# Pairs of tiles in one DMA for the branch products, block work in single steps, and an earlier start of the next sums' loads

## The chip, the cores and the metric

The kernel runs on one core of a Trainium2 chip. The metric is device time in microseconds (us) of one execution, smaller is better. The engines of the core run side by side, each in its own order: TensorE (PE: matmuls), VectorE (DVE), ScalarE (ACT), GpSimd (POOL) and SyncE (SP), whose queue issues all DMAs of this kernel. An instruction waits on its engine until all it depends on is done, and all that stand behind it wait too.

## What is computed

One layer of a streaming encoder, for 2048 prompt frames and 64 frames of a running stream: an input projection, a differential attention branch, a retention branch, gates, and an output part. The change touches the output part only, which is in the reference:

```python
oa = (rmsnorm(oa, subln_g) * (1.0 - lam_init)).reshape(B, T, W_A) * jax.nn.silu(za)
ob = rmsnorm(ob).reshape(B, T, W_B) * jax.nn.silu(zb)
m = ga * (oa @ w_oa) + gb * (ob @ w_ob)
return x + m @ w_out
```

`oa`, `ob`, `za`, `zb` have 512 columns for 2112 rows, `ga` and `gb` (sigmoids) and `m` 1024 columns, `w_out` is 1024 x 1024. All is float32: each operand is split into a high and a low part, and each product takes three matmuls (high x high, high x low, low x high).

## The kernel before

A planner writes the program. Every piece of work is a generator (a task) with a priority; `loop` runs the task with the lowest priority number among those that are due by the planner's own estimates, `self.pe` being the planned time of TensorE. `yield t` means "go on when TensorE has reached t", `yield lambda: ...` "when this holds", `take`/`give` hand out buffers with the time from which they are free. The order in which tasks emit instructions is the static order of each engine. `ld` (L135) and `st` (L140) are DMAs on SyncE.

The part around the change, in the order of the program:

- **Scratch.** Earlier stages write transposed results to DRAM: `oaT`, `obT` (the branches before their gate), `zaT`, `zbT`, and the merge gates `gaT`, `gbT`.
- **Branch products**, the stage from 1575 to 1773 us. The 2112 rows are cut into 8 groups (g) of 264 columns (`GW`). For each branch (br 0 and 1) and each of four tiles kt of 128 channels, `out_prep` loads the two tiles `on` and `z` (132 KB each) into two of 11 "oz" buffers; `og_fin` does silu on ScalarE (L1664), the product on POOL (L1667), the high part `ogh` on ScalarE (L1677) and the low part `ogl` on VectorE (L1680). The buffer of `z` is given back after the product, that of `on` after the low part. Of `ogh` and `ogl` there are three sets of 4 tiles, so a set can be written only when TensorE is through with the set three before it.
- `m_tile` then makes one of eight tiles (ct) of 128 output channels: 12 matmuls for branch a into a "mm" bank, 12 for branch b into an "s" bank (L1722 to L1724). There are two banks of each. Tile ct of group g needs two gates: `gates` loads them into two of 10 "gt" buffers, `gate` takes tanh on ScalarE (L1698), `m_fin` multiplies both banks with them on VectorE (the eviction, L1742), adds them on POOL (L1746) and stores the sum `mT` (132 KB). One gt buffer is given back after the add, the other when the store is planned to have landed.
- **Weights of the products**: `load_wo` loads 128 x 256 pieces, `split_fin` splits them (L1610, L1613, L1617).
- **Block work for the last matrix.** `w_out` is cut into four block rows c, and the last product uses seven products P1 to P7 of sums of blocks instead of eight of blocks. `b_prep` loads four raw tiles for each c (`b_raw`, 256 KB each), forms the sums t1 to t4 on VectorE (L1758) and splits blocks and sums (`b_split`: casts L1815 on ScalarE, subtractions L1818 on VectorE). The sums of c = 2, 3 are split late (`b_late`), when the buffers of the first product weights come free in group 7. All this runs beside the branch products, on ScalarE and VectorE. `out_prep` waits ahead of the loads of group 1 until the first four raw loads are out (`b_left < 13`).
- **The last matrix**, from 1773 us: for each of 8 groups `y_load` loads four tiles `a` of `mT`, `y_prep` forms the sums s1 to s4 (s1, s2 on VectorE, s3, s4 on POOL) and splits them into `ah` (L1853) and `al` (L1860); `y_group` multiplies (L1934) in the order P1, P2, P6, P5, P7, P3, P4; `y_out` copies banks to `u` (L1962), adds the residual and stores (L1984). For the first group, loads of `a11` and `a12` come early; the others follow when t4 of all four c is split.

Of the kernel before, what the change touches and what calls it, by code (L numbers as in the profile page):

```python
# [8 lines left out]
F32 = mybir.dt.float32  # L9
# [23 lines left out]
BUFS = {"thi": 1, "tlo": 2, "ev": 3, "q": 2, "K": 4, "V": 4, "ath": 2, "atl": 2,  # L33
        "ws": 3, "w": 12, "r_o": 1, "r_sq": 1, "r_y": 1, "r_hi": 1, "r_lo": 1, "state": 2,
        "mm": 2, "s": 2, "at": 2, "pv": 1, "tp": 1,
        "oz": 11, "og": 16, "ob": 8, "gt": 10, "wa": 16, "st": 13, "ac": 16, "u": 9, "xt": 10}
LAT = 250.0
SLACK = 400.0
PACE = 700.0
# [20 lines left out]
class Hybrid:  # L60
# [91 lines left out]
    def scratch(self):  # L152
        tc = self.tc
        self.qT = [tc.dram_tile([4, 128, TT], F32, name=f"qT{i}") for i in range(2)]
        self.kT = [tc.dram_tile([4, 128, TT], F32, name=f"kT{i}") for i in range(2)]
        self.vN = [tc.dram_tile([TT, 512], F32, name=f"vN{i}") for i in range(2)]
        self.vsN = tc.dram_tile([NS, 512], F32, name="vsN")
        self.vbN = tc.dram_tile([TT, 512], F32, name="vbN")
        self.qbT = tc.dram_tile([4, 128, TT], F32, name="qbT")
        self.kbT = tc.dram_tile([4, 128, TT], F32, name="kbT")  # L160
        self.zaT = tc.dram_tile([4, 128, 8 * GW], F32, name="zaT")
        self.zbT = tc.dram_tile([4, 128, 8 * GW], F32, name="zbT")
        self.gaT = tc.dram_tile([8, 128, 8 * GW], F32, name="gaT")
        self.gbT = tc.dram_tile([8, 128, 8 * GW], F32, name="gbT")
        self.oaT = tc.dram_tile([4, 128, 8 * GW], F32, name="oaT")
        self.obT = tc.dram_tile([4, 128, 8 * GW], F32, name="obT")
        self.mT = tc.dram_tile([8, 128, 8 * GW], F32, name="mT")

    def consts(self):
# [1436 lines left out]
    def split_fin(self, tag, h, l, s, t, on_pool, slot, key):  # L1606
# [12 lines left out]
        self.give(tag, t)  # L1619
        slot[key] = t  # L1620

    def load_wo(self, br, q):
        csl = slice(256 * (q % 2), 256 * (q % 2) + 256)
        for kt in range(4):
            hl, slot = self.wo[br][kt]
            h, l = hl[q // 2]
            yield from self.take("oz")
            s = self.sb(self.z3p, [128, GW], "oz", "wst")[:, :256]
            t = self.ld(s, self.i[("w_o_diff", "w_o_ret")[br]][0, 128 * kt:128 * kt + 128, 256 * q:256 * q + 256],
                        1 << 17)  # L1630
            self.spawn(self.split_fin("oz", h[:, csl], l[:, csl], s, t, (kt + q) % 3 == 0, slot, q), 2)
            yield self.pe

    def out_prep(self):
        pa = self.z3p
        self.wo = [[([[self.sb(self.zq, [128, 512], "wa", "woq", F32R) for n in "hl"],
                      [pa.tile([128, 512], F32R, tag=f"wo{n}{br}{kt}", name=f"wo{n}{br}{kt}") for n in "hl"]], {})
                    for kt in range(4)] for br in range(2)]
        for br in range(2):
            yield from self.load_wo(br, 0)  # L1640
        for g in range(8):
            gsl = slice(GW * g, GW * g + GW)
            for br, (oT, zT) in enumerate(((self.oaT, self.zaT), (self.obT, self.zbT))):
                for kt in range(4):
                    yield from self.take("oz", 2)
                    on = self.sb(pa, [128, GW], "oz", "on")
                    z = self.sb(pa, [128, GW], "oz", "z")
                    self.ld(z, zT[kt][:, gsl], 1 << 17)
                    t = self.ld(on, oT[kt][:, gsl], 1 << 17)
                    og = []  # L1650
                    self.ogs.append(og)
                    self.spawn(self.og_fin(on, z, t, og, (2 * g + br) % 3 == 2), 1)
                    yield self.pe
            if g == 0:
                self.spawn(self.gates(), 0)
                for q in range(1, 4):
                    for br in range(2):
                        yield from self.load_wo(br, q)
                yield lambda: self.b_left < 13

    def og_fin(self, on, z, t, og, third):
        nc = self.nc
# [3 lines left out]
        yield t  # L1666
        nc.gpsimd.tensor_mul(on, on, z)  # L1667
        t = self.G(GW, t)
        self.give("oz", t)
        tag = "ob" if third else "og"  # L1670
        yield from self.take(tag, 2)
        pool = self.z4 if third else self.z3p
# [62 lines left out]
    def m_fin(self, g, ct, pss):  # L1735
# [9 lines left out]
        yield t  # L1745
        nc.gpsimd.tensor_add(gs[0], gs[0], gs[1])  # L1746
# [428 lines left out]
    def run(self):  # L2175
# [20 lines left out]
        self.b_left = 16  # L2196
        for k in ("ac", "u", "xt", "ob"):
            self.res[k].free = []
        self.q_end = self.smx = None
# [96 lines left out]
```

## Time and profile before

| | us |
|---|---|
| median of 3 runs | 1947.14 |
| fastest and slowest of them | 1945.34, 1948.15 |
| the profiled execution | 1945.82 |
| its span | 1944.0 |
| branch products in it | 1574.90 to 1773.03 |
| last matrix in it | 1773.03 to the end |

The stages of the tail, each row a stretch: length, then the busy time of TensorE, its weight loads, VectorE, ScalarE and POOL, with the instructions; then the granted TensorE clock (1.00 is full speed), the busy share of the DMA engines, and GB/s.

```
1531.00:1575.00 44.00, 44.00 (x196) 36.44 (x195) 21.32 (x36) 25.78 (x64) 21.03 (x24) 1.00 0.89 273
1575.00:1599.00 24.00, 23.21 (x189) 22.83 (x188) 18.93 (x29) 12.20 (x31) 15.82 (x17) 1.00 0.66 203
1599.00:1624.00 25.00, 24.81 (x204) 24.61 (x203) 18.18 (x34) 14.67 (x35) 16.48 (x18) 1.00 0.87 265
1674.00:1699.00 25.00, 24.37 (x196) 23.81 (x195) 11.07 (x26) 14.89 (x37) 12.84 (x17) 1.00 0.88 258
1723.00:1747.00 24.00, 23.72 (x192) 23.33 (x192) 10.09 (x25) 11.69 (x28) 8.31 (x11) 1.00 0.60 168
```

How to read the views below: a row of the timeline has start, length, engine, line, operation, `out<-in`, shapes, and in brackets the idle time just before it and what ended it. In the list of waits, `<-` names the last releaser. `mm`, `s` and `at` are PSUM banks, `woh`/`woq` product weights, `bh`/`bl` and `bht`/`blt` high and low parts of blocks and of block sums.

### The profile page before, as it was taken

The numbers are of one execution on the slowest core, as the hardware profiler recorded it, in microseconds if no ns is written. First come the engines' busy times: TensorE is split into PE (matmuls) and PEld (weight loads), VectorE is DVE, ScalarE is ACT, GpSimd is POOL, SyncE is SP. The second block draws the span as 40 slices with busy tenths as digits, with TensorE's granted clock in tenths as the row PEclk, the third lists the DMA queues.
The fourth block names the chain that finished last, engine by engine and source line by source line (L and its number), as shares of the span: only waits on it lengthen the run. The fifth ranks groups of instructions, "written<-read, shape, count | busy, mean of one in ns | idle before, by whom it ended". The sixth has DMA issues, their size and how long they took to land.

```text
span 1944.0 us, 33842 instructions
## 1 busy us (share of the span) xinstructions
PE 1927.5 (99%) x11984; PEld 1731.2 (89%) x11984; DVE 1166.6 (60%) x2798; ACT 964.9 (50%) x2072; POOL 490.1 (25%) x429
## 2 busy tenths in 40 slices
PE   9999999999999999999999999999999999999999
PEld 8779999999988899999998888888888889998887
DVE  6753777646666336648856757845773376545643
ACT  7443766544434235535765646544563445653321
POOL 4310112112122121211121111112113356543422
PEclk9999999999999999999999999999999999999999
DMA  7747454335566655654344253363133678866651
GB/s 235 240 151 199 143 143 132 106 102 156 163 192 187 166 148 168 202 183 141 112 120 128 76 146 96 99 185 116 63 99 108 190 229 259 264 196 189 190 151 65
DMA packets 372074, 303.32 MB, mean 156 GB/s; under 512 B 77440, under 2 KB 334720, under 8 KB 371904
## 3 DMA queue, kind: packets, MB, share of 16 engines
q1 hardware_dynamic: 371904, 301.16, 52.6%
q8 instruction: 94, 1.54, 0.4%
q14 instruction: 76, 0.62, 0.1%
HBM read 195.87 MB, written 100.14 MB: 152 GB/s over the span
## 4 chain that ended last, share of the span: by engine, by line
PE 88%; DVE 5%; DMA 3%; POOL 1%; issue 1%; ACT 1%; SPq 1%; DVEq 0%; POOLq 0%; ACTq 0%
PE mm L554 51%; PE mm L1934 4%; PE s L1052 3%; PE s L1053 3%; PE at L1160 3%; PE at L1934 2%; PE pv L1139 2%; PE pv L1140 2%; PE pv L1138 2%; PE s L1934 1%; PE s L1723 1%; PE s L1724 1%; PE pv L1521 1%; PE mm L1723 1%; PE s L1722 1%
## 5 line engine op out<-in xcount | busy, mean ns | idle before, releaser
L514 POOL TENSOR_TENSOR wl<-ws,wh 128x512 fp32r<-128x512 f32 x191 | 261.4, 1380 | 896.2 <-ACT wh L504 544.9
L554 PE MATMUL mm<-xh,wh 128*128 128x512 f32 (+2 forms) x1280 | 460.7, 360 | 0.0
L554 PE MATMUL mm<-xh,wl 128*128 128x512 f32 (+2 forms) x1280 | 452.7, 354 | 0.0
L554 PE MATMUL mm<-xl,wh 128*128 128x512 f32 (+2 forms) x1280 | 451.9, 353 | 0.0
L554 PEld LDWEIGHTS mm<-xh,wl 128*128 128x128 f32 x1280 | 241.0, 188 | 31.7
L554 PEld LDWEIGHTS mm<-xh,wh 128*128 128x128 f32 x1280 | 241.4, 189 | 29.1 <-issue 0.2
L554 PEld LDWEIGHTS mm<-xl,wh 128*128 128x128 f32 x1280 | 241.6, 189 | 27.8
L554 PE MATMUL mm<-wh,xh 128*128 128x256 f32 (+1 forms) x768 | 236.7, 308 | 0.0
L554 PE MATMUL mm<-wh,xl 128*128 128x256 f32 (+1 forms) x768 | 231.3, 301 | 0.0
L554 PE MATMUL mm<-wl,xh 128*128 128x256 f32 (+1 forms) x768 | 231.0, 301 | 0.0
L1175 DVE TENSOR_TENSOR atl<-at,ath 128x512 fp32r<-128x512 f32 (+1 forms) x144 | 93.7, 659 | 136.2 <-ACT ath L1173 136.1
L504 ACT CAST wh<-ws 128x512 fp32r<-128x512 f32 x192 | 117.0, 617 | 112.6 <-PE mm L554 90.3
L1091 ACT ACTIVATE row<-row,a_mx 128x1024 f32<-128x1024 f32 (+7 forms) x160 | 153.7, 962 | 24.5 <-DVE a_mx L1071 24.3
L554 PEld LDWEIGHTS mm<-wh,xh 128*128 128x128 f32 x768 | 146.3, 190 | 7.1 <-issue 0.5
L554 PEld LDWEIGHTS mm<-wl,xh 128*128 128x128 f32 x768 | 146.4, 191 | 6.7 <-issue 0.5
L554 PEld LDWEIGHTS mm<-wh,xl 128*128 128x128 f32 x768 | 146.3, 190 | 5.5
L865 DVE TENSOR_TENSOR ev<-mm,rsb 128x512 f32<-128x512 f32 x140 | 83.0, 593 | 112.8 <-PE mm L554 112.4
L1173 ACT CAST ath<-at 128x512 fp32r<-128x512 f32 (+1 forms) x144 | 78.7, 563 | 141.5 <-PE at L1160 138.4
L1061 DVE CUSTOM_DVE_ANT_0 row<-s,dfar 128x512 f32<-128x512 f32 (+2 forms) x192 | 118.2, 630 | 46.4 <-PE s L1053 45.9
L1052 PE MATMUL s<-K,q 128*128 128x512 f32 (+3 forms) x320 | 118.4, 374 | 0.7 <-DVE a_acc L1061 0.7
L1053 PE MATMUL s<-K,q 128*128 128x512 f32 (+3 forms) x320 | 115.2, 362 | 0.0
L1110 ACT ACTIVATE row<-row,a_w 128x1024 f32<-128x1024 f32 (+4 forms) x96 | 85.1, 898 | 34.4 <-DVE a_w L1105 31.2
(342 smaller groups left out, 4193.5 us busy)
## 6 DMA issues: line engine op xcount, KB each, us to landing
ws<-in_w_in_dram SPq DMA_DIRECT2D x192, 256.0 KB, 3.1
q<-qT SPq DMA_DIRECT2D x128, 128.0 KB, 3.0
V<-vN SPq DMA_DIRECT2D x24, 512.0 KB, 5.4
K<-kT SPq DMA_DIRECT2D x48, 256.0 KB, 4.3
a<-mT SPq DMA_DIRECT2D x34, 256.0 KB, 4.1
gt<-gaT SPq DMA_DIRECT2D x64, 132.0 KB, 3.2
gt<-gbT SPq DMA_DIRECT2D x64, 132.0 KB, 3.1
mT<-gt SPq DMA_DIRECT2D x64, 132.0 KB, 3.0
```

What stands on the lines that cost most here:

```text
L504: self.nc.scalar.copy(h, st)
L514: self.nc.gpsimd.tensor_sub(l, st, h.bitcast(F32))
L554: nc.tensor.matmul(ps, p, q, start=c == 0 and i == 0, stop=c == KC - 1 and i == 2)
L865: nc.vector.tensor_mul(ev, ps, rsb)
L1052: nc.tensor.matmul(ps, q1s, kk, start=True, stop=False)
L1053: nc.tensor.matmul(ps, q2s, kk, start=False, stop=True)
L1061: nc.vector.tensor_tensor_reduce(out=units[k0 // 1024][:, k0 % 1024:k0 % 1024 + n], in0=ps, in1=tab, scale=-SLOPES[h], scalar=3.0e38, op0= ...
L1091: nc.scalar.activation(u, u, AF.Exp, bias=mx, scale=-1.0, accum_out=lp[:, k:k + 1])
L1110: nc.scalar.activation(u1, u1, AF.Identity, scale=w[:, 1:2])
L1173: nc.scalar.copy(ah[:, :w], at[:, :w])
L1175: nc.vector.tensor_sub(al[:, :w], at[:, :w], ah[:, :w].bitcast(F32))
L1934: nc.tensor.matmul(q[b], u, v, start=fresh and c == 0 and m == 0, stop=c == 3 and m == 2, skip_group_check=True)
```

## The change

Three edits go together.

1. The scratch of each branch and of the gates is interleaved (`ozT`, `gT`), so that `on` and `z` of a tile come by one DMA of 264 KB into one double buffer, and both gates too. Buffers: 5 doubles for 11 singles ("oz"), 5 doubles for 10 singles ("gt"). An oz double is given back after the low part, a gt double after the store. The product weights come two pieces to a DMA.
2. `b_raw`, `b_prep` and `b_fin` (for c < 2) yield until 1500 ns of planned TensorE time have passed after each step. The wait on `b_left` goes.
3. `y_load` starts when t1 of three c is split, instead of t4 of all four.

```diff
-        "oz": 11, "og": 16, "ob": 8, "gt": 10, "wa": 16, "st": 13, "ac": 16, "u": 9, "xt": 10}
+        "oz": 5, "og": 16, "ob": 8, "gt": 5, "wa": 16, "st": 13, "ac": 16, "u": 9, "xt": 10}
...
+        self.ozT = [tc.dram_tile([4, 128, 2, 8 * GW], F32, name=f"ozT{br}") for br in range(2)]
+        self.gT = tc.dram_tile([8, 128, 2, 8 * GW], F32, name="gT")
+        (self.oaT, self.zaT), (self.obT, self.zbT) = ([[t[h][:, k] for h in range(4)] for k in range(2)]
+                                                      for t in self.ozT)
+        self.gaT, self.gbT = ([self.gT[c][:, k] for c in range(8)] for k in range(2))
...
-        for kt in range(4):
-            hl, slot = self.wo[br][kt]
-            h, l = hl[q // 2]
+        for k2 in range(2):
             yield from self.take("oz")
-            s = self.sb(self.z3p, [128, GW], "oz", "wst")[:, :256]
-            t = self.ld(s, self.i[("w_o_diff", "w_o_ret")[br]][0, 128 * kt:128 * kt + 128, 256 * q:256 * q + 256],
-                        1 << 17)
+            s = self.sb(self.z3p, [128, 2, GW], "oz", "wst")[:, :, :256]
+            t = self.ld(s, self.i[("w_o_diff", "w_o_ret")[br]][0, 256 * k2:256 * k2 + 256, 256 * q:256 * q + 256]
+                        .rearrange("(c p) n -> p c n", p=128), 1 << 18)
...
-                    yield from self.take("oz", 2)
-                    on = self.sb(pa, [128, GW], "oz", "on")
-                    z = self.sb(pa, [128, GW], "oz", "z")
-                    self.ld(z, zT[kt][:, gsl], 1 << 17)
-                    t = self.ld(on, oT[kt][:, gsl], 1 << 17)
+                    yield from self.take("oz")
+                    both = self.sb(pa, [128, 2, GW], "oz", "oz")
+                    t = self.ld(both, self.ozT[br][kt][:, :, gsl], 1 << 18)
...
-                yield lambda: self.b_left < 13
...
         t = self.G(GW, t)
-        self.give("oz", t)
...
-            yield from self.take("gt", 2)
-            pair = [self.sb(self.z3p, [128, GW], "gt") for _ in range(2)]
-            for gt, gT in zip(pair, (self.gaT, self.gbT)):
-                t = self.ld(gt, gT[ct][:, GW * g:GW * g + GW], 1 << 17)
-            self.spawn(self.gate(n, ct, pair, t), 0)
+            yield from self.take("gt")
+            both = self.sb(self.z3p, [128, 2, GW], "gt")
+            t = self.ld(both, self.gT[ct][:, :, GW * g:GW * g + GW], 1 << 18)
+            self.spawn(self.gate(n, ct, [both[:, br] for br in range(2)], t), 0)
...
         t = self.G(GW, t)
-        self.give("gt", t)
         yield t
         t = self.st(self.mT[ct][:, GW * g:GW * g + GW], gs[0], 1 << 17)
         self.give("gt", t)
...
-            self.b_left -= 1
-        yield t + 600
+            yield self.pe + 1500
+        if t + 600 > self.pe:
+            yield t + 600
...
             t1 = self.add(False, ALU.subtract, raw["t1"], raw["12"], raw["11"], self.pe)
+            yield self.pe + 1500
             for k in ("11", "21", "22"):
                 t = yield from self.b_split(k, c, raw[k], self.pe)
+                yield self.pe + 1500
...
-            yield t3
+            yield max(t3, self.pe + 1500)
...
-            yield t2
+            yield max(t2, self.pe + 1500)
...
             self.give("st", t)
+            if c < 2:
+                yield self.pe + 1500
...
-        yield lambda: len(self.wt["t4"]) == 4
+        yield lambda: len(self.wt["t1"]) > 2
```

TensorE's instructions and their order are the same in both programs, and the other engines have as many as before, but for SyncE, which issues 1410 DMAs instead of 1554: 64 fewer for the gates, 64 for `on` and `z`, 16 for weights. The order of the others differs from about 1527 us on.

ScalarE at the boundary of groups 1 and 2, before (`gt<-gt,bg` is a tanh, `z<-z` a silu, `ogh<-on` the high part that TensorE needs at the boundary, `bht` a block sum's):

```order
L1698 ACTIVATE gt<-gt,bg 128x264 x2
L1664 ACTIVATE z<-z 128x264
L1815 CAST bht_18301<-wst 128x512
L1815 CAST bht_18299<-wst 128x512
L1698 ACTIVATE gt<-gt,bg 128x264 x2
L1815 CAST bht_18303<-wst 128x512
L1677 CAST ogh<-on 128x264 x8
L1664 ACTIVATE z<-z 128x264
```

The same place on ScalarE in the changed program, where `oz<-oz` is the silu and `ogh<-oz` the high part:

```order
L1818 CAST bht_18259<-wst 128x512
L1665 ACTIVATE oz<-oz 128x264
L1697 ACTIVATE gt<-gt,bg 128x264 x6
L1677 CAST ogh<-oz 128x264 x5
L1697 ACTIVATE gt<-gt,bg 128x264 x4
L1665 ACTIVATE oz<-oz 128x264 x2
```

The silu and three block casts that stood within the last steps ahead of the high parts stand earlier now, and six tanhs in a row stand there instead.

SyncE ahead of the same boundary, before, from the stores of tiles 12 and 13 on (`mT<-gt` is the store of a tile, `gt<-gaT` and `gt<-gbT` gate loads):

```order
L140 DMA mT<-gt 128x264 x2
L135 DMA z<-zbT 128x264
L135 DMA on<-obT 128x264
L135 DMA gt<-gaT 128x264
L135 DMA gt<-gbT 128x264
L135 DMA gt<-gaT 128x264
L135 DMA gt<-gbT 128x264
L140 DMA mT<-gt 128x264
```

And in the changed program on SyncE, from the store of tile 12 on, with one load for both gates:

```order
L140 DMA mT<-gt 128x264
L135 DMA gt<-gT 128x2x264
L140 DMA mT<-gt 128x264
L135 DMA gt<-gT 128x2x264
L140 DMA mT<-gt 128x264
L135 DMA oz<-ozT_67 128x2x264 x2
L135 DMA gt<-gT 128x2x264
```

The gate load of tile 17 now stands directly behind the store of tile 12, whose buffer it takes, and that of tile 18 directly behind the store of tile 13; before, the loads stood further behind the stores whose buffers they took.

VectorE at the start of the last matrix, before, from the last two tiles' evictions (`gt<-gt,mm` and `gt<-gt,s`) on; `a<-a` are the sums s1 and s2, `al<-a,ah` low parts, `u<-s,u` an output sum:

```order
L1742 SCALAR_TENSOR_TENSOR gt<-gt,mm 128x264
L1742 SCALAR_TENSOR_TENSOR gt<-gt,s 128x264
L1742 SCALAR_TENSOR_TENSOR gt<-gt,mm 128x264
L1742 SCALAR_TENSOR_TENSOR gt<-gt,s 128x264
L1758 TENSOR_TENSOR a<-a 128x512 x2
L1860 TENSOR_TENSOR al<-a,ah 128x512
L1984 TENSOR_TENSOR u<-s,u 128x512
L1860 TENSOR_TENSOR al<-a,ah 128x512 x4
L1984 TENSOR_TENSOR u<-mm,u 128x512
```

VectorE there in the changed program, from the third last tile's evictions' end on:

```order
L1821 TENSOR_TENSOR wot<-wst,wot 128x512
L1756 TENSOR_TENSOR a<-a 128x512
L1741 SCALAR_TENSOR_TENSOR gt<-gt,mm 128x264
L1741 SCALAR_TENSOR_TENSOR gt<-gt,s 128x264
L1756 TENSOR_TENSOR a<-a 128x512
L1741 SCALAR_TENSOR_TENSOR gt<-gt,mm 128x264
L1741 SCALAR_TENSOR_TENSOR gt<-gt,s 128x264
L1863 TENSOR_TENSOR al<-a,ah 128x512 x5
L1987 TENSOR_TENSOR u<-s,u 128x512
L1987 TENSOR_TENSOR u<-mm,u 128x512
```

Both sums of the first group stand ahead of the last evictions, and five low parts ahead of the first output sum. On POOL the two sums s4 and s3 of that group now stand ahead of the add of the last tile (L1745); before, they stood behind it and behind the first residual add.

More of the change, by code (lines that the diff above doesn't have):

```diff
@@ L160, in scratch @@
         self.kbT = tc.dram_tile([4, 128, TT], F32, name="kbT")
[L161 to L166, printed above, removed]
+        self.ozT = [tc.dram_tile([4, 128, 2, 8 * GW], F32, name=f"ozT{br}") for br in range(2)]
[3 more added lines that the diff above has]
+        self.gaT, self.gbT = ([self.gT[c][:, k] for c in range(8)] for k in range(2))
         self.mT = tc.dram_tile([8, 128, 8 * GW], F32, name="mT")
@@ L1604, in ret_sample, with split_fin @@
         self.state, self.t_state = None, 0.0
-    def split_fin(self, tag, h, l, s, t, on_pool, slot, key):
+    def split_fin(self, tag, h, l, s, t, on_pool, slot, key, box):
         nc = self.nc
@@ L1618, in split_fin @@
             t = self.V(n + 120, t)
-        self.give(tag, t)
+        box.append(t)
+        if len(box) == 2:
+            self.give(tag, max(box))
         slot[key] = t
@@ L1623, in load_wo @@
         csl = slice(256 * (q % 2), 256 * (q % 2) + 256)
-        for kt in range(4):
-            hl, slot = self.wo[br][kt]
-            h, l = hl[q // 2]
+        for k2 in range(2):
             yield from self.take("oz")
-            s = self.sb(self.z3p, [128, GW], "oz", "wst")[:, :256]
-            t = self.ld(s, self.i[("w_o_diff", "w_o_ret")[br]][0, 128 * kt:128 * kt + 128, 256 * q:256 * q + 256],
-                        1 << 17)
-            self.spawn(self.split_fin("oz", h[:, csl], l[:, csl], s, t, (kt + q) % 3 == 0, slot, q), 2)
+            s = self.sb(self.z3p, [128, 2, GW], "oz", "wst")[:, :, :256]
+            t = self.ld(s, self.i[("w_o_diff", "w_o_ret")[br]][0, 256 * k2:256 * k2 + 256, 256 * q:256 * q + 256]
+                        .rearrange("(c p) n -> p c n", p=128), 1 << 18)
+            box = []
+            for u in range(2):
+                kt = 2 * k2 + u
+                hl, slot = self.wo[br][kt]
+                h, l = hl[q // 2]
+                self.spawn(self.split_fin("oz", h[:, csl], l[:, csl], s[:, u], t, (kt + q) % 3 == 0, slot, q, box), 2)
             yield self.pe
@@ L1642, in out_prep @@
             gsl = slice(GW * g, GW * g + GW)
-            for br, (oT, zT) in enumerate(((self.oaT, self.zaT), (self.obT, self.zbT))):
+            for br in range(2):
                 for kt in range(4):
-                    yield from self.take("oz", 2)
-                    on = self.sb(pa, [128, GW], "oz", "on")
-                    z = self.sb(pa, [128, GW], "oz", "z")
-                    self.ld(z, zT[kt][:, gsl], 1 << 17)
-                    t = self.ld(on, oT[kt][:, gsl], 1 << 17)
+                    yield from self.take("oz")
+                    both = self.sb(pa, [128, 2, GW], "oz", "oz")
+                    t = self.ld(both, self.ozT[br][kt][:, :, gsl], 1 << 18)
                     og = []
                     self.ogs.append(og)
-                    self.spawn(self.og_fin(on, z, t, og, (2 * g + br) % 3 == 2), 1)
+                    self.spawn(self.og_fin(both[:, 0], both[:, 1], t, og, (2 * g + br) % 3 == 2), 1)
                     yield self.pe
@@ L2195, in run @@
         self.wt = {k: [] for k in BLOCKS}
-        self.b_left = 16
         for k in ("ac", "u", "xt", "ob"):
```

## The prediction

> **What bounds the kernel now.** I read the page's span, busy row and chain first, then what TensorE waits for, then its instructions at the starts of the groups.
>
> ```profile
> span 1944.0 us, 33842 instructions
> PE 1927.5 (99%) x11984; PEld 1731.2 (89%) x11984; DVE 1166.6 (60%) x2798; ACT 964.9 (50%) x2072; POOL 490.1 (25%) x429
> PE 88%; DVE 5%; DMA 3%; POOL 1%; issue 1%; ACT 1%; SPq 1%; DVEq 0%; POOLq 0%; ACTq 0%
> ```
>
> TensorE is busy 99% of the span and carries 88% of the chain. Since the change leaves every TensorE instruction in its place, it can only remove or add TensorE waits. All rows of the order ahead of about 1527 us stay too; what counts is the tail: the branch products (1575 to 1773 us) and the start of the last matrix. The list of TensorE's waits from 1540 us on (engine, line, releaser: us in total, times, longest) is short:
>
> ```profile
> PE s L1723 <- DVE ogl L1680: 3.0, 6, 1.7
> PE s L1722 <- ACT ogh L1677: 1.1, 1, 1.1
> PE at L1934 <- DVE al L1860: 1.1, 1, 1.1
> PE mm L1722 <- DVE gt L1742: 0.8, 1, 0.8
> PE mm L1934 <- ACT u L1962: 0.7, 1, 0.7
> ```
>
> That is 3.0 + 1.1 + 0.8 = 4.9 us in the products and 1.1 + 0.7 = 1.8 us in the last matrix. The true loss is larger, as the group starts in the timeline show (start, length):
>
> ```profile
> 1574.90 0.29 PE L1722 MATMUL mm<-ogh,woq 128*128 128x264 f32 x1
> ...
> 1599.54 0.28 PE L1722 MATMUL mm<-ogh,woq 128*128 128x264 f32 x1
> ...
> 1623.35 0.29 PE L1722 MATMUL mm<-ogh,woq 128*128 128x264 f32 x1
> ...
> 1652.85 0.28 PE L1722 MATMUL mm<-ogh,woq 128*128 128x264 f32 x1
> ...
> 1749.64 0.28 PE L1722 MATMUL mm<-ogh,woq 128*128 128x264 f32 x1
> ...
> 1770.10 0.29 PE L1722 MATMUL mm<-ogh,woh 128*128 128x264 f32 x1
> ...
> 1773.03 0.40 PE L1934 MATMUL mm<-bh,ah 128*128 128x512 f32 x1
> 1773.26 0.40 PE L1934 MATMUL mm<-bl,ah 128*128 128x512 f32 x1
> ```
>
> Group 7 runs undisturbed: seven tiles from 1749.64 to 1770.10 are 2.923 us a tile, 23.38 us a group. Group 0 takes 24.64 (1.26 lost), group 1 23.81 (0.43), group 2 29.50 (6.12), groups 3 to 6 together 96.79 (3.26). Lost: 11.1 us. Group 0 shows that a wait of 0.8 in the list costs about 0.4 more until the pipeline is full again. In group 2 the clock adds its part; columns are the stretch, its length, busy times, then granted clock, DMA share, GB/s:
>
> ```profile
> 1624.00:1650.00 26.00, 23.22 (x165) 22.81 (x165) 18.84 (x34) 15.66 (x39) 15.59 (x17) 0.87 0.82 250
> ...
> 1747.00:1770.00 23.00, 23.00 (x191) 23.00 (x191) 14.70 (x28) 11.88 (x26) 7.10 (x8) 1.00 0.57 159
> ```
>
> A granted clock of 0.87 over 26 us is 3.4 us of lost work behind waits of 1.1 and 1.7 us: those two cost 6.1 in all. The Trainium skill ("TensorE: Matmul & The Clock Gate", Part 1) has the clock halved after at least one idle window of about 3.4 us; this trace differs, the waits being shorter and 0.4 us of work lying between them. By that rule the long stall would cost only its 2.8 us of waiting.
>
> **The change part by part.**
>
> *Block steps give way.* In group 0 the eviction that TensorE waits for stands behind four operations of 1 us each on VectorE:
>
> ```profile
> 1586.73 1.24 DVE L1818 TENSOR_TENSOR bl<-wst,bh 128x512 fp32r<-128x512 f32 x1
> 1587.89 1.24 DVE L1758 TENSOR_TENSOR wst<-wst 128x512 f32<-128x512 f32 x1
> 1589.05 0.98 DVE L1680 TENSOR_TENSOR ogl<-on,ogh 128x264 fp32r<-128x264 f32 x1
> 1589.96 0.41 DVE L1742 SCALAR_TENSOR_TENSOR gt<-gt,mm 128x264 f32<-128x264 f32 x1
> ```
>
> In the new order one block step, 1.24 at most, lies between two tiles' evictions, and a tile lasts 2.92: a pair of evictions (0.82) plus 1.24 fits. I take 1.0 of the 1.26 as gone (bounds 0 and 1.26). The cover that is given up: two adds now stand just ahead of group 1's first ogl operations, 2.5 us in a place with about 1.5 to spare; bounds for the start of group 1 are 0 and 1.3 lost against 0.43 now. I leave it at 0.4.
>
> *The boundary of groups 1 and 2.* It is late on ScalarE and then on VectorE:
>
> ```profile
> 1622.90 0.42 ACT L1664 ACTIVATE z<-z 128x264 f32<-128x264 f32 x1 [1.32 <-DMA z<-zaT]
> ...
> 1625.59 2.60 ACT L1677 CAST ogh<-on 128x264 fp32r<-128x264 f32 x8
> ...
> 1627.12 3.60 DVE L1680 TENSOR_TENSOR ogl<-on,ogh 128x264 fp32r<-128x264 f32 x7
> ```
>
> The casts stand behind a silu that idles 1.32 for a load and behind four block casts and tanhs; the first ogl ends 1628.10, where it should have been ready at about 1623.35 + 1.5 = 1624.9. In the changed order six tanhs and then five ogh casts follow each other, with no silu or block cast between, and the ogl alternate with evictions. The casts can begin when the last tile of the group before has freed the buffers, 2.9 ahead of the boundary, and are needed 1.5 behind it: 4.4 us for four casts at 0.33, 1.3, the first subtraction at 0.51 (3.60 by 7) and one pair of evictions at 0.82; the other three subtractions are needed 0.37 apart and fall a little behind. I keep 0.5 of the 6.12 (bounds 0 and 6.1).
>
> *One load for two tiles.* SyncE issues 144 loads fewer and moves the same bytes. What this is worth stands at the other boundaries, where the tanh ahead of the casts waits for a gate:
>
> ```profile
> 1724.41 0.52 ACT L1698 ACTIVATE gt<-gt,bg 128x264 f32<-128x264 f32 x1 [2.32 <-DMA gt<-gbT]
> ```
>
> The loads' medians from issue to landing in this stretch (name, count, KB, us):
>
> ```profile
> mT<-gt SPq DMA_DIRECT2D x62, 132.0 KB, 3.0
> gt<-gaT SPq DMA_DIRECT2D x59, 132.0 KB, 3.2
> ...
> wst<-in_w_out_dram SPq DMA_DIRECT2D x16, 256.0 KB, 4.7
> ```
>
> A pair should land like the 256 KB block load, after 4.7, so 1.5 later than a single load, while issuing takes one place instead of two. The chain for the first gate of the next group goes: tile 3 ends, evictions and POOL add 1.85 (below, 1774.88 against the last product's end at 1773.03), issue 0.4, store 3.0, issue 0.4, load 4.7, two tanhs at 0.5, together 11.35. From the end of tile 3 to the boundary are four tiles, 11.7: the tanhs end 0.35 before it, against a need of about 0.7 behind it. That holds with 1 to spare, so I expect these boundaries to be shortened, not all cured: 2.0 of the 3.26 in groups 3 to 6 stay (bounds 0 and 3.3). The weight loads that are paired as well end before the products, where TensorE passes from the projections at 1574.90 without a wait: 0 (0 to 0.4). The fewer oz buffers, five pairs held until the subtraction instead of eleven singles, let four pairs of one branch and one of the next lie ready; the next four are needed a whole branch later, so I price this at 0, and at the 0.4 of a short wait per boundary if that cover were gone.
>
> *The last matrix starts with its sums done.* Before:
>
> ```profile
> 1773.79 1.09 POOL L1746 TENSOR_TENSOR gt<-gt 128x264 f32<-128x264 f32 x1 [2.17 <-DMA mT<-gt]
> ...
> 1776.80 0.59 ACT L1962 COPY u<-mm 128x512 f32<-128x512 f32 x1 [11.26 <-DMA mT<-gt]
> ...
> 1781.18 0.69 DVE L1984 TENSOR_TENSOR u<-s,u 128x512 f32<-128x512 f32 x1 [2.49 <-POOL u L1756]
> 1781.79 1.14 DVE L1860 TENSOR_TENSOR al<-a,ah 128x512 fp32r<-128x512 f32 x1
> ...
> 1781.10 2.96 POOL L1756 TENSOR_TENSOR a<-a 128x512 f32<-128x512 f32 x2
> ```
>
> The fourth product waits 1.1 for the al that stands behind an output sum; the fifth 0.7 for a copy behind casts. In the new order the al operations stand ahead of that sum and both sums of the first group lie between the last evictions, so both waits go. In exchange two POOL sums (2.96) now stand ahead of the POOL add of the very last tile. It ends about 3.1 after the products instead of 1.85, and as the copy of u waits for that tile's store (row above: released by the store, 3.8 after 1773.03), the copy moves to about +5.0, the cast of the third product's operand to +6.1 and its rest to +6.8. The third product is due at +5.45 (two products of twelve matmuls at 0.23): a new wait of 0.6 to 1.3, with the refill about 1.2. Old loss 1.8 + 0.6 refill = 2.4; gain 1.2 (bounds 0.5 and 1.8). Eight low parts of the block work lie between the last evictions:
>
> ```profile
> 1768.04 1.86 DVE L1818 TENSOR_TENSOR wot<-wst,wot 128x512 fp32r<-128x512 f32 x2
> ```
>
> At 0.93 each they were split 3, 3 and 2 between tiles and are now 4, 3 and 1, with the two sums behind them. The longest piece, 3.7 and a pair of evictions at 0.82, is 1.6 over a tile, and the next adds 0.7; TensorE has a second pair of banks, a whole tile of 2.9, as cover: 0.1 (0 to 1.0).
>
> *Sum.* Lost before: 11.1 + 2.4 = 13.5. Left: 0.3 + 0.4 + 0.5 + 2.0 + 1.2 + 0.1 = 4.5. Gain 9.0. The profiled execution took 1945.82 us, so 1936.8; the median of the runs, 1947.14, lies 1.3 higher: **1938**.
>
> **The rivals.**
>
> *The long stall stays (1944, chance 0.17).* A tanh whose pair lands late holds the casts at one boundary by 2 us or more, and the clock halves again. For it: tanhs of the next group still stand ahead of the casts, and the row at 1724.41 shows 2.3 us of idleness for one. Against: the 1 us to spare above. Of the 6.1 the forecast has kept 0.5, so 1938 + 5.6.
>
> *SyncE becomes serial (1962, chance 0.16; this is the slower side).* A gate load must wait until the store five tiles back has landed, and everything behind it on SyncE, the next store above all, waits too. In the changed order 15 of the 59 such loads stand directly behind that store, 10 two rows, 10 three and 13 four rows behind. The quiet end of the stage of before has such a queue (first what SyncE waits for in the whole stage, then its issues there):
>
> ```profile
> SPq L135 <- DMA mT<-gt: 20.4, 19, 1.9
> ...
> 1736.44 0.42 SPq L140 DMA_DIRECT2D mT<-gt  x1
> 1736.95 0.38 SPq L135 DMA_DIRECT2D gt<-gaT  x1
> 1738.55 0.32 SPq L135 DMA_DIRECT2D gt<-gbT  x1
> ```
>
> There the store landed after 1.7 and a cycle lasted 2.5. With 3.0, the median of the stage, and 0.45 per row between (0.42 and 0.38 long above, with a little between them), the waits add up to 15 x 3.0 + 10 x 2.55 + 10 x 2.1 + 13 x 1.65 + 11 at about 1.0, or 124 us; with the 200 issues that the order has there, at 0.45, that is 214 us for a stage that lasts 198 now: 16 slower, less the 1.2 of the last matrix. With 1.7 it is 51 + 90 = 141, hidden under TensorE's 64 x 2.923 = 187. It decides from a landing of about 2.5 on, and costs against before from 2.7 on. I take 2.2, since a queue that waits has fewer transfers under way; the 3.0 was measured with 40 issues a group instead of 24. The Trainium skill ("DMA: Bandwidth & Descriptors", Anatomy of one DMA) speaks of a fixed 2.0 us plus bytes by 436 GB/s, an estimate of 2.3 for the store that more bytes per load do not shorten. By it the queue stays just below the point where it decides; the trace has both smaller and larger.
>
> *The boundaries don't care (1940, chance 0.15).* The freed issue slots aren't what held groups 3 to 6 and group 0; only the long stall and the last matrix get better: 5.6 + 1.2 = 6.8 less, so 1940.3 with the offset.
>
> **How the numbers follow.** Forecast 0.52, the rivals 0.17, 0.16 and 0.15. 0.2% of the time, 3.9 us, is about what a measurement of this kernel can tell from no change. Faster than 1943.2: forecast and third rival, 0.67. Slower than 1951: 0.14 of the serial queue, the rest of it within. Same: 0.19. The low end takes all bounds at their best, 13.5 - 0.9 less and no offset: 1933. The high end covers the first rival with the offset of the runs and the serial queue in part: 1950.
>
> **What would show it.** Right: the list of waits has no row above 1 us in the products; the granted clock is 1.00 in every stretch; group 2 lasts about 24; the fourth product waits for nothing and the third up to 1.3 for ah or al of the first group. The store's landing should lie near 2.2, with SyncE waiting for stores in many more than 19 places, none of which reaches TensorE. Wrong: evictions that wait for tanhs in the middle of a group (the serial queue), or a clock below 1 behind a boundary (the long stall). If the third product waits for over 2 us, the price of the POOL sums was too low.

## The result and the profile after

| | before | changed |
|---|---|---|
| median, us | 1946.79 (4 runs) | 1970.72 (4 runs) |
| lowest to highest | 1945.34 to 1948.15 | 1970.22 to 1973.09 |
| span of the profiled execution | 1944.0 | 1971.3 |
| start of the branch products | 1574.90 | 1574.22 |
| branch products (first product to first P1) | 198.1 | 224.9 |
| last matrix to the end | 171.0 | 172.2 |

The changed kernel is slower: ratio 1.0126, 95% interval 1.0110 to 1.0142. The forecast was 1938, faster. The medians lie 23.9 us apart; the two profiled executions lie 27.3 apart, as the changed kernel's was the longest of its four. Of these 27.3 us, 26.7 are in the products, 1.2 in the last matrix and -0.7 ahead of both. Figures by stage below are those of the profiled executions.

What TensorE waits for from 1520 us on in the changed kernel (engine, line, releaser: us in total, times, longest):

```profile
PE mm L1721 <- DVE gt L1741: 9.2, 6, 1.8
PE s L1721 <- ACT ogh L1677: 6.1, 4, 2.3
PE mm L1937 <- DVE gt L1741: 3.4, 1, 3.4
PE s L1722 <- DVE ogl L1680: 3.0, 10, 0.4
PE mm L1937 <- ACT ah L1856: 1.3, 1, 1.3
```

The row for gt, an eviction that TensorE waits for, was one wait of 0.8 in group 0 and is now six waits inside groups; `ogh`, the cast at a boundary, is late four times instead of once. The group starts in the timeline (first matmuls of groups 1, 2 and 3) show where it begins:

```profile
1597.48 0.29 PE L1721 MATMUL mm<-ogh,woq 128*128 128x264 f32 x1
...
1621.29 0.28 PE L1721 MATMUL mm<-ogh,woq 128*128 128x264 f32 x1
...
1652.59 0.28 PE L1721 MATMUL mm<-ogh,woq 128*128 128x264 f32 x1
```

Group 0 (from 1574.22) takes 23.26, no loss at all; group 1 23.81, 0.43 lost as before; group 2 31.30, 7.9 lost against 6.1 before, and every group behind it loses 3 to 8 (the last one with the wait of 3.4 ahead of the first P1). The stretches of that part (length; busy TensorE, weight loads, VectorE, ScalarE, POOL; granted clock, DMA share, GB/s):

```profile
1575.00:1602.00 27.00, 27.00 (x225) 27.00 (x224) 15.69 (x35) 12.64 (x31) 13.20 (x16) 1.00 0.66 203
1602.00:1630.00 28.00, 25.95 (x193) 24.94 (x192) 13.74 (x29) 13.67 (x34) 14.18 (x17) 0.94 0.68 214
1630.00:1658.00 28.00, 25.40 (x188) 24.34 (x187) 15.36 (x30) 15.51 (x37) 13.51 (x15) 0.94 0.68 194
1658.00:1690.00 32.00, 28.79 (x216) 27.63 (x215) 14.91 (x31) 15.64 (x38) 14.58 (x17) 0.95 0.70 213
1690.00:1715.00 25.00, 20.08 (x158) 19.25 (x157) 12.00 (x23) 11.16 (x30) 11.56 (x14) 1.00 0.79 232
```

VectorE, ScalarE and POOL are less busy per us than before, and so are the DMA engines (0.67 over all the products, where 0.76 stood): nothing is short of throughput. A clock of 0.94 over 28 us is 1.7 us lost; there are five such falls in the products.

What SyncE waits for from 1530 to 1800 us, the first two rows:

```profile
SPq L135 <- DMA mT<-gt: 78.4, 47, 4.2
SPq L140 <- POOL gt L1745: 16.3, 13, 2.9
```

The first row, loads that wait until a store has landed, was 20.4 us in 19 waits in the products of the kernel before. How that hurts is seen on SyncE ahead of the boundary of groups 3 and 4 (start, length; L135 are loads, L140 stores; a wait lies ahead of the start):

```profile
1674.23 0.59 SPq L140 DMA_DIRECT2D mT<-gt  x1
1677.59 0.52 SPq L135 DMA_DIRECT2D gt<-gT  x1
1678.22 0.54 SPq L140 DMA_DIRECT2D mT<-gt  x1
1681.31 0.52 SPq L135 DMA_DIRECT2D gt<-gT  x1
1681.89 0.59 SPq L140 DMA_DIRECT2D mT<-gt  x1
1685.17 0.53 SPq L135 DMA_DIRECT2D gt<-gT  x1
1685.80 0.55 SPq L140 DMA_DIRECT2D mT<-gt  x1
```

and on POOL, whose adds these stores take away:

```profile
1673.13 0.76 POOL L1745 TENSOR_TENSOR gt<-gt 128x264 f32<-128x264 f32 x1
...
1674.56 0.76 POOL L1745 TENSOR_TENSOR gt<-gt 128x264 f32<-128x264 f32 x1
...
1676.47 0.75 POOL L1745 TENSOR_TENSOR gt<-gt 128x264 f32<-128x264 f32 x1
1677.63 1.14 POOL L1745 TENSOR_TENSOR gt<-gt 128x264 f32<-128x264 f32 x1 [0.40 <-DVE gt L1741]
```

The adds end at 1673.89, 1675.32, 1677.22 and 1678.77; their stores are issued 0.3, 2.9, 4.7 and 7.0 later. From the second on, each store is ready but stands behind a gate load, and that load waits for the landing of the store just ahead of it: the store's issue takes 0.6, it is 2.8 until the load can start (1674.82 to 1677.59), and the load's issue takes 0.5. A cycle lasts 3.7 to 4.0 where TensorE takes 2.92 a tile, so the lag grows until the gates run out. At the boundary this reaches TensorE through ScalarE, whose casts of the next group stand behind a tanh (timelines of ScalarE and TensorE):

```profile
1681.02 0.92 ACT L1697 ACTIVATE gt<-gt,bg 128x264 f32<-128x264 f32 x2 [2.88 <-DMA gt<-gT]
1681.84 1.33 ACT L1677 CAST ogh<-oz 128x264 fp32r<-128x264 f32 x4
...
1682.29 0.39 PE L1721 MATMUL s<-ogh,woq 128*128 128x264 f32 x1 [0.88 <-ACT ogh L1677]
```

The gate load of 1677.59 lands, only then does the tanh ahead of the casts run, at 1681.02, and TensorE, which is due, waits 0.88.

### The profile page after: what moved, and what is told of

Same layout as the page of the kernel before. It is cut to its first block, busy times and chain, and to the rows that moved or that the text cites. A ratio compares the mean times of both kernels' runs of the same rounds, so it can differ in the third digit from the quotient of the medians.

```text
span 1971.3 us, 33708 instructions
## 1 busy us (share of the span) xinstructions
PE 1937.7 (98%) x11984; PEld 1736.5 (88%) x11984; DVE 1160.8 (59%) x2798; ACT 962.2 (49%) x2072; POOL 486.4 (25%) x429
## 4 chain that ended last, share of the span: by engine, by line
PE 85%; DMA 6%; DVE 4%; ACT 2%; issue 1%; POOL 1%; SPq 1%; DVEq 0%; ACTq 0%; POOLq 0%
PE mm L553 50%; PE mm L1937 5%; PE s L1051 3%; PE s L1052 3%; PE at L1159 3%; PE at L1937 2%; DMA gt<-gT 2%; PE pv L1138 2%; PE pv L1139 2%; PE pv L1137 2%; DMA mT<-gt 1%; DMA oz<-ozT 1%; PE s L1937 1%; PE pv L1520 1%; PE tp L733 1%
```

## The experiments

The theory, S: a gate double is held until its store has landed; its next load stands right behind that store on SyncE; later stores and loads stand behind the load, and the lag feeds itself. Rivals: O, five oz doubles held to the low part are too few; B, the block steps that give way bring a worse order; H, the gate doubles are simply held too long, wherever the load stands.

Medians in us; ratio to the kernel before, run beside it, with 95% interval; length of the products, and SyncE's waits for the landing of a store from 1570 to 1800 us (us, times), from each profile. For the faster kernels that stretch takes in the start of the last matrix: the single waits of e8, e12, e14 and e15 lie there.

| run | median | ratio | products | waits |
|---|---|---|---|---|
| before | 1946.79 | | 198.1 | 21.8, 20 |
| changed | 1970.72 | 1.0126 (1.0110 to 1.0142) | 224.9 | 78.4, 47 |
| e1 gates single | 1952.17 | 1.0030 (1.0018 to 1.0042) | 204.4 | 48.8, 40 |
| e2 oz single | 1974.27 | 1.0145 (1.0130 to 1.0161) | 220.2 | 73.1, 46 |
| e3 no pairs | 1947.70 | 1.0002 (0.9992 to 1.0011) | 197.2 | 38.6, 37 |
| e4 own store buffers | 1937.63 | 0.9956 (0.9941 to 0.9970) | 191.7 | none |
| e5 pairs only | 1968.87 | 1.0109 (1.0094 to 1.0124) | 219.0 | 75.7, 39 |
| e6 early loads only | 1947.37 | 1.0006 (0.9997 to 1.0015) | 198.3 | 26.1, 20 |
| e7 store on POOL | 1956.84 | 1.0048 (1.0031 to 1.0065) | 205.9 | 110.3, 48 |
| e8 e4 without edits 2, 3 | 1942.90 | 0.9985 (0.9974 to 0.9995) | 190.6 | 1.3, 1 |
| e9 SyncE order, all | 1974.83 | 1.0154 (1.0139 to 1.0170) | 195.5 | 29.0, 29 |
| e10 before, SyncE order, all | 1983.33 | 1.0193 (1.0177 to 1.0209) | 196.6 | 0.5, 1 |
| e11 e3 + own buffers | 1937.53 | 0.9960 (0.9945 to 0.9975) | 191.6 | 0.4, 1 |
| e12 before + own buffers | 1951.42 | 1.0029 (1.0017 to 1.0042) | 198.6 | 1.3, 1 |
| e13 SyncE order, tail | 1939.84 | 0.9969 (0.9958 to 0.9980) | 193.3 | 28.8, 29 |
| e14 before, SyncE order, tail | 1949.23 | 1.0020 (1.0010 to 1.0029) | 198.8 | 2.4, 1 |
| e15 e4 + SyncE order, tail | 1938.11 | 0.9960 (0.9945 to 0.9975) | 190.8 | 1.3, 1 |
| e16 e3 + SyncE order, tail | 1938.05 | 0.9963 (0.9950 to 0.9976) | 190.3 | 4.7, 6 |

**Which part.** e1 takes the gate pairs back, e2 the oz and weight pairs, e3 both:

```diff
# e1, on the changed kernel
-        "oz": 5, "gt": 5
+        "oz": 5, "gt": 10
-            yield from self.take("gt")
-            both = self.sb(self.z3p, [128, 2, GW], "gt")
+            yield from self.take("gt", 2)
+            pair = [self.sb(self.z3p, [128, GW], "gt") for _ in range(2)]
# e2, the same for on, z and the weights; e3, both
```

> The changed kernel with the gates loaded singly again (two loads of 132 KB into two of 10 buffers, one given back after the POOL add); the pairs of on and z, the block steps and the early loads stay. Theory S (serial gate loads: a pair is held until its store has landed, its load stands right behind that store on SyncE, and the next store behind the load): 1935 to 1946, SyncE waits for stores under 30 us in the products, no TensorE wait for gt over 1 us. Rival O (five oz doubles held until the low part are too few): 1962 to 1972. Rival B (the block steps that give way bring tanhs and evictions into a worse order): 1960 to 1972.

> The changed kernel with on, z and the product weights loaded singly again into 11 buffers; the gate pairs, the block steps and the early loads stay. Theory S: 1962 to 1980 (the gate cycle is untouched and SyncE has 80 more issues), SyncE waits for stores over 60 us. Rival O: under 1950. Rival B: 1960 to 1972.

> Both loads single again, all buffers as before; only the block steps that give way, the wait on raw loads that is gone, and the early loads of the last matrix remain of the change. Theory S: 1935 to 1947, SyncE waits for stores under 30 us. Rival O: the same. Rival B: 1960 to 1975.

Single gates win back 18.6 of the 23.9 us, single oz loads nothing: O falls, and since e3, with the block steps in, is level with before, B falls too. But e1 stays 6 above what was expected and still waits 48.8 us for stores, and e3 waits 38.6 where under 30 was expected (its time, 1947.70, lies just above its range): single gates shorten the chain and do not end it. Why e1 is slower than e3 by 4.5 was not followed up.

e5 and e6 are edits 1 and 3 alone:

> Edit 1 alone: all loads in pairs with 5 doubles each; block work, its wait and the start of the last matrix's loads as before. Theory S: 1958 to 1975, the loss is in the pairs, SyncE waits for stores over 60 us. If the loss needs the block steps too (another order on ScalarE and VectorE): under 1950.

> Edit 3 alone on the kernel before: the loads of the last matrix start when t1 of three block rows is split. The products are untouched: within 1944 to 1948; the wait of the fourth product for al gone, at most 1.3 us new in the third.

The pairs alone cost 23.1 over before, nearly the whole loss. The early loads alone are worth nothing that can be told (interval 0.9997 to 1.0015): the fourth product's wait went, and the third had a new one of 1.8, where 1.3 at most was expected.

**The buffer.** e4 keeps every pair and lets the POOL add write into a buffer of its own, so that no gate load waits for a store:

```diff
-        "oz": 5, "og": 16, "ob": 8, "gt": 5,
+        "oz": 5, "og": 16, "ob": 8, "gt": 4, "mo": 3,
...
-        nc.gpsimd.tensor_add(gs[0], gs[0], gs[1])
+        yield from self.take("mo")
+        mo = self.sb(self.z3p, [128, GW], "mo")
+        nc.gpsimd.tensor_add(mo, gs[0], gs[1])
         t = self.G(GW, t)
+        self.give("gt", t)
         yield t
-        t = self.st(self.mT[ct][:, GW * g:GW * g + GW], gs[0], 1 << 17)
-        self.give("gt", t)
+        t = self.st(self.mT[ct][:, GW * g:GW * g + GW], mo, 1 << 17)
+        self.give("mo", t)
```

> The changed kernel, all pairs kept, but the POOL add writes into one of 3 buffers of its own, from which the store goes; there are 4 gate doubles, given back after the add. A gate load then waits for the add of the tile four back, not for a store's landing. Theory S: 1935 to 1948, SyncE waits for stores under 15 us in the products. If pairs as such are the trouble (their later landing, SyncE's longer issues) or rivals O or B: 1960 and more.

The median is 1937.63, faster than both kernels, as the changed kernel had been forecast to be. TensorE's waits from 1540 us on in e4, complete, and SyncE's longest:

```profile
PE mm L1721 <- DVE gt L1741: 2.1, 3, 1.0
PE s L1722 <- DVE ogl L1680: 0.9, 3, 0.4
PE mm L553 <- POOL wl L513: 0.2, 1, 0.2
...
SPq L135 <- POOL mo L1747: 50.8, 39, 3.6
```

SyncE still waits 50.8 us, now for adds, so the sum of its waits decides nothing. What e4 takes away is the loop: no gate load waits for a store's landing, and a store starts 0.61 behind its add in the median, where it was 2.57 in the changed kernel. But e4 differs from the changed kernel in more than the buffer: the planner gets the gate buffers back earlier and puts ScalarE, VectorE and POOL into another order too.

**The place on SyncE.** e7 moves only the stores to POOL's queue (`self.st(...)` becomes `nc.gpsimd.dma_start(...)`, the order of the other engines kept; 13 of the 64 gate loads stand one or two loads further up or down on SyncE):

> The changed kernel with the 64 stores of the product tiles issued by POOL, right behind its add, instead of by SyncE; buffers, pairs and the order of all else are kept, and a gate load still waits for the landing of the store five back. Theory S, in which the harm comes of the next store standing behind a waiting gate load: 1936 to 1952, TensorE waits for gt under 3 us in all. If holding the gate double until the landing is itself too long (a rival, H): 1962 and more. POOL's own issue of a DMA is not in any trace here; if it costs 1 us or more for each, POOL stays under 2.9 a tile all the same.

In the products 19.0 of the 26.7 us come back (205.9 against 224.9 and 198.1). The median lies 5 us above the range of theory S and 5 below that of H, and TensorE's waits for gt are 4.1 us where under 3 was expected. The stores now follow their adds by 0.4 in the median, but the gate loads still wait on SyncE for landings, 110.3 us in all, with oz loads behind them. So stores that stand behind a waiting load are a large part of the harm and not all of it; what is left in e7 was not followed further.

The section on the kernel before says that the order in which tasks emit instructions is that of each engine. For SyncE this is wrong: `manual_schedule` names TensorE, ScalarE, VectorE and POOL, and where a DMA stands on SyncE is left to the scheduler that builds the program. It moved the gate loads up to their stores. So the same DMAs can be put in the emitted order, in which the planner leaves each store its time to land:

```diff
# e9 and e10, whole program
-    return {ET.PE, ET.Activation, ET.DVE, ET.Pool}
+    return {ET.PE, ET.Activation, ET.DVE, ET.Pool, ET.SP}
# e13 to e16, from the loads of the product weights on, in out_prep
+        self.reg.enter_context(self.tc.manual_schedule(engines={mybir.EngineType.SP}))
```

> The changed kernel with one more engine in the set whose order is kept by hand: SyncE now issues its DMAs in the order in which the tasks emit them. Same DMAs, sizes and buffers; the gate loads stand 3 rows or more behind the store they wait for (25 at 3, none at 1 or 2) instead of 15 at 1 and 10 at 2. Theory S, the load right behind its store is what makes the chain: 1938 to 1955, SyncE waits for stores at least halved against 78 us. If the place on SyncE does not matter (H, the gate double is held too long): 1962 and more.

> The kernel before with SyncE in the emitted order, as the counterpart of the run above: what the order does by itself over the whole program. Theory S: between 1940 and 1952, since few of its gate loads stand close behind a store in either order.

Both totals missed the expectation, by 20 and 31 us. The products are short (195.5 and 196.6), but they start some 33 us later in both runs. The time is lost far ahead of them, in projections (e9, waits of TensorE); what in the new order holds these up was not followed further:

```profile
PE mm L553 <- ACT raw L785: 13.7, 1, 13.7
PE mm L549 <- ACT raw L826: 10.4, 1, 10.4
```

So e13 and e14 keep the old order up to the products:

> The changed kernel with SyncE in emitted order from the loads of the product weights on; the order ahead of that is the changed kernel's. Theory S: products 194 to 198 us long as in e9, total 1943 to 1951. If the early loss of e9 had given the tail its slack: products over 205, total over 1955.

> The kernel before with the same: products 195 to 199 us (e10: 196.6), total 1943 to 1949, so that the place on SyncE matters only where gate loads stand close behind their stores.

e13 has all edits, sizes and buffers of the changed kernel, and its TensorE, ScalarE, VectorE and POOL run the same rows in the same order. It is 31 us faster than the changed kernel, 3 below its expected range, and faster than before: 0.9969, interval 0.9958 to 0.9980. For the kernel before the same order on SyncE brings nothing (e14, 1.0020; 1949.23 is just above the expected 1949). All that TensorE waits for in e13 from 1540 us on is this:

```profile
PE s L1723 <- DVE ogl L1681: 2.5, 8, 0.4
```

SyncE and POOL ahead of the boundary of groups 3 and 4 in e13 (1671.87):

```profile
1670.87 0.33 SPq L140 DMA_DIRECT2D mT<-gt  x1
1671.52 0.53 SPq L135 DMA_DIRECT2D gt<-gT  x1
1672.91 1.54 SPq L135 DMA_DIRECT2D oz<-ozT  x2
1674.55 0.55 SPq L140 DMA_DIRECT2D mT<-gt  x1
...
1669.71 1.14 POOL L1746 TENSOR_TENSOR gt<-gt 128x264 f32<-128x264 f32 x1 [1.93 <-DVE gt L1742]
1673.70 0.82 POOL L1746 TENSOR_TENSOR gt<-gt 128x264 f32<-128x264 f32 x1 [2.85 <-DVE gt L1742]
```

Here the stores go 0.02 and 0.03 behind the ends of their adds (1670.85, 1674.52). Over all 64 tiles the store starts behind its add's end by 0.03 in the median and by over 2 once in e13, by 2.57 and 35 times in the changed kernel. H falls: the doubles are held for a landing as before. The lag by itself does not tell the loss: e3, level with before, has 2.45 and 39 times. But there too it costs time, since e16, the same single loads with the other order, has 0.55 and 10 times and is 9.7 us faster. e13 moves all of SyncE's rows in the tail and not the gate loads alone, so it shows that the order does it, and by the rows above how, but not that no other move has a share. What a store takes from issue to landing has hardly changed (views of the DMAs in the products, changed kernel, then e13; name, count, KB, median us from the start of the issue):

```profile
mT<-gt SPq DMA_DIRECT2D x53, 132.0 KB, 3.4
```

```profile
mT<-gt SPq DMA_DIRECT2D x63, 132.0 KB, 3.3
```

**One cause, two cures; and the pairs.**

> Pairs, block steps, early loads, 3 store buffers of their own, and SyncE in emitted order from the products on. One cause, two cures: 1936 to 1940, as with the store buffers alone (1937.6). Two causes: under 1936.

> Single loads with the buffers of before, block steps and early loads, SyncE in emitted order from the products on. Theory S: 1936 to 1944, as the loads stand 3 and mostly 5 or more rows behind their stores (no pairs in the other order: 1947.7). If pairs are needed to free SyncE: 1944 to 1950.

> Single loads (10 oz and 8 gt buffers), block steps and early loads as in the changed kernel, 3 store buffers of their own. If the release at the add is all that counts: 1936 to 1941, like the pairs with store buffers (1937.6). If the pairs' fewer issues on SyncE are worth something once the chain is gone: 1941 to 1947.

> Edit 1 with the three store buffers of their own and 4 gate doubles, without the block steps and without the early loads. Theory S: 1938 to 1946; what it is slower than the run with all three edits and store buffers (1937.6) is the worth of the block steps and the early loads, 1 to 8 us.

> The kernel before with 3 store buffers of their own (10 oz and 8 gt buffers), nothing else. If pairs are worth nothing: like the pairs alone with store buffers (1942.9), 1940 to 1945. If a busy SyncE is what holds the boundaries: 1944 to 1949.

e15, with both cures, is no faster than e4: they mend one thing. e11 and e16, with single loads, end level with e4 and e13, so beside the block steps the pairs are worth nothing. Without the block steps they seem to be worth something: e8 is 8.5 faster than e12, which has neither. The block steps and early loads together bring 5.3 with pairs (e8 to e4) and 13.9 without (e12 to e11). Part of both is one wait of 3.8 for al at the start of the last matrix (1.1 in the kernel before), which e8 and e12 have and e4 and e11 have not; and as the planner also gives each of these four programs another order on ScalarE, VectorE and POOL, the differences are not the worth of single edits. e12 missed its expectation; at 1951 it is slower than before, with that wait and two of 2.0 and 1.7 at the boundary of groups 2 and 3. Of all versions e11 (1937.53), e4, e16 and e15 are the fastest and can't be told apart.

## Why the prediction was wrong

- **The bound** was right: only TensorE's waits in the tail changed, and the clock behind them.
- **Block steps** came out as forecast in number. Group 0 lost 1.26 and now loses nothing (1.0 of it was taken as gone); group 1 loses 0.43 (0.4 taken). The steps alone do not secure it: with the same steps group 0 loses 0.9 in e4 and 4.2 in e11.
- **The step that failed** is the one on the serial queue: "I take 2.2, since a queue that waits has fewer transfers under way". The 1.7 beside it was counted from the end of the store's issue, the 3.0 from its start. Counted from the end, the landing was 2.8 in the median of the products (3.4 from the start). That is beyond both marks of the working: about 2.5, where the queue decides, and 2.7, where it costs against before. The figure of 2.0 us plus bytes that the prediction took from the Trainium skill ("DMA: Bandwidth & Descriptors", Anatomy of one DMA) is a fit for DMAs that GpSimd issues, as that section says. The stores of both kernels are SyncE's, and the estimate of 2.3 from it was below the 2.6 (before) and 2.8 (changed) measured.
- **The slower rival** had the mechanism, its place and its sign (evictions that wait for tanhs inside a group, which reached TensorE six times), and was given 0.16. Its size was short. Its price, 1962, was 9 short of the median, and its 214 us for the products are 224.9. With a landing of 2.8 in place of 3.0 the same sum gives only about 203. It had counted no loss to the clock, which is about 1.7 in each of five falls, 0.45 for an issue that took 0.53 in the median, and no lag that one store hands on to the next. What each of the three is worth was not separated beyond the clock's share.
- **The same step spoiled the boundary's chain.** It went "evictions and POOL add 1.85", "issue 0.4", "store 3.0" and on to 11.35 against 11.7, as if the store were issued when its add ended. A store behind a waiting load is issued up to 7.4 later. So the one of spare was gone from group 2 on, although a pair of gates landed after 3.4 and not after the 4.7 of the chain; group 2 lost 7.9 where 0.5 was left in the sum, and groups 3 to 6 lost 21.2 where 2.0 was.
- **The other rival at that place**, the clock that halves behind a late tanh (1944), also happened, but as a consequence of the lag: in e4 and e13 the clock is 1.00 over all the products.
- **The last matrix** was half right. The third product waits 1.3 for ah (0.6 to 1.3 taken), the fourth for nothing. The first product's wait of 3.4 for the last evictions was not foreseen; it goes with the lag, as e4 and e13 have no such wait. The stage itself is 1.2 longer, where 1.2 shorter was forecast; it has one more fall of the clock (1.7). In e4 and e13 it is 2.2 and 1.8 shorter than before.
- **The rest of the sum** was nearly right. With the lag cured, the gain over the kernel before, run beside it, is 8.6 in e4 and 5.9 in e13, where 9.0 was forecast. In e13 the last matrix is better than taken, but group 1 loses 1.5 (0.4 taken) and groups 3 to 6 lose 4.7 (2.0 taken). The store's landing in e13 is 3.3 from the issue's start, so the landing alone does not decide either; 25 of its gate loads stand 3 rows behind their store and none nearer, where 25 of the changed kernel's stood 1 or 2 rows behind.

## What to carry to other kernels

When a buffer's next load waits for a store of the same buffer, and both go through one in-order queue, look at what stands between the two and what stands behind the load: if issue, landing and issue together exceed the period of the work, the lag grows with each turn, even where no engine and no DMA is short of time. Give the store a buffer of its own, or put the load some rows further back; to issue only the stores elsewhere cured a part here. Count the period with the landing measured in the loaded stage, from the same point each time, and check which engines' order the program really fixes.

## What the hardware showed that was not expected

The clock fell behind a wait shorter than many that left it alone. In the changed kernel it halved behind the wait of 0.88 at 1682.29 (the stretch 1658 to 1690 above has 0.95). A longer wait did nothing (a row of TensorE's timeline, and the stretch around it):

```profile
1755.56 0.39 PE L1721 MATMUL mm<-ogh,woh 128*128 128x264 f32 x1 [1.72 <-DVE gt L1741]
```

```profile
1742.00:1770.00 28.00, 24.64 (x196) 23.78 (x195) 11.01 (x25) 12.15 (x32) 11.54 (x15) 1.00 0.73 203
```

Each fall in the products cost about 1.7 us, that is some 3.4 us at half clock. The Trainium skill ("TensorE: Matmul & The Clock Gate", Part 1) has a free-running window of about 3.4 us that decides on the clock. The traces agree with it: their records of the clock show every change, in all 18 traces, a whole number of 3.41 us behind the first, so the windows can be laid over TensorE's idle times. Between 1560 and 1830 us no window had to be idle as a whole: all 23 windows at full clock in which TensorE idled 1.79 us or more in sum were followed by one at half clock, 5 of the 22 with 1.22 to 1.75, and none with less. The window of the wait of 0.88 holds 1.42 in several waits. That of the wait of 1.72 holds no more than this wait; both lie in the band where either happens, and what tells them apart no run here shows.

Emptying the queue did not make stores fast: with the DMA engines busy 0.67 of the time instead of 0.76, the median of the stores' landing rose from 3.0 to 3.4 (from 2.6 to 2.8 when counted from the end of the issue). In the stretch shown, a store was issued right behind a gate pair each time, and landed 0.3 to 0.4 behind it, 2.5 to 2.7 after the end of its own issue; in the quiet end of the kernel before 1.7 was measured behind single loads. The size of the load ahead was not varied by itself.
